# Gather steps beside the gates: from the streamed blocks and ticks to two behind each gate piece

## The chip, the core and the metric

The kernel runs on one core of a Trainium2 chip. TensorE (PE) does matrix products and transposes, VectorE (DVE) and ScalarE (ACT) the elementwise work, GpSimd (POOL) issues the gathers, SyncE (SP) and ACT issue the other transfers. Each engine takes its instructions in the order in which the program holds them, and waits where one of them needs something that another engine or a transfer has not yet delivered. The metric is the time of one execution on the device in microseconds (us), of which the median of three runs is compared.

## What is computed

Two layers of a decoder work on 512 prompt tokens and 64 sample tokens of width 1024. A layer is a mixer (a gated recurrence beside a short convolution, after one input projection and before one output projection) and a retrieval block, which is what the change touches. Cut to that block:

```
def peer(h, w_q, sub_keys, u_tab, v_tab):          # per 128 tokens
    q = (xb @ w_q).reshape(tb, PEER_HEADS, 2, D_KEY_HALF)
    s = jnp.einsum('thpd,hpkd->thpk', q, sub_keys)
    sv, si = lax.top_k(s, TOPK)
    ...
    fv, fi = lax.top_k(cand, TOPK)
    idx = jnp.take_along_axis(cand_idx, fi, axis=-1)     # 8 heads x 16 of 16384 experts
    g = jax.nn.softmax(fv, axis=-1)
    act = jax.nn.gelu(jnp.einsum('thkd,td->thk', u_tab[idx], xb))
    return jnp.einsum('thk,thkd->td', g * act, v_tab[idx])

    x = x + g1[:, None, :] * (merged @ w_out)
    x = x + g2[:, None, :] * peer(hn2, peer_w_q, peer_sub_keys, peer_u, peer_v)
```

Every token takes 128 of 16384 rows of a table u, forms a dot product with each, and adds up 128 rows of a table v with the weights that come of it. Both tables are 64 MB for a layer.

## The kernel before, in words

The tokens go two ways. For 384 prompt tokens the block is **dense**: all 16384 rows of u and of v are streamed as 128 blocks of 128 rows, the products of all rows with all tokens are formed, and a gate matrix that is zero outside the chosen rows picks what counts. The other 128 prompt tokens and the 64 sample tokens are **gathered**: a step fetches 128 rows of 4 KB by their indices with one indirect transfer that POOL issues (L659, tiles urs and vrs for the samples, urp and vrp for the prompt tokens, all of one ring of five buffers), and one DVE instruction uses them: a dot product (L665) or a weighted sum (L681; the first of a sum at L679). A layer has 64 + 64 steps of the samples and 128 + 128 of the prompt tokens, and behind the last sum stands finish (pf, L733, and x, L736), which adds the result to the stream x.

The retrieval block of a layer has these stages:

- the queries, and then the **u stage**: 72 streamed blocks, lo_u_0 to lo_u_71. Each block is split into a high and a low part (hi on ACT at L132, lo on DVE at L133) and multiplied by PE (pu, L712, 24 products). Three buffers hold raw pairs of blocks, four the parts.
- within the u stage, beside the stream, dense_slots turns the top-k lists into slots (three calls of combine, all DVE), and phase_a forms the gate matrix in 24 gate pieces of 4 quarters. A quarter is two DVE comparisons (oh, L944), two DVE products (A, L949), eight PE products (pgm, L954) and a copy (stg, L956); a piece ends with a transfer to DRAM (gd, L958), which ACT issues. In layer 0 the weights of the next layer's modulation are streamed in the same stage (raw_ada, pm).
- phase_b: 128 blocks of v (lo_v), the first 56 of which with a block of u each (lo_ub). Per block DVE applies the gates (L1047, from gt, read back from gd) and splits the result (h2l, L1050), and PE forms 18 products (pvo, L1018). The products of the last four blocks are held back to the end.
- the **tail**: the queue of gather steps is flushed, then finish, the sums of squares (L223), the transposed output (pyt, L1072) and its addition to x (L1075). In layer 0 the next mixer follows, whose projection weights are lo_wi; in layer 1 the last norm and y (L1109).

The gather steps stand in a queue, gtasks. pump(n) adds n to a credit and issues a step for each whole unit; issue_after(anchor[0]) places the step's DVE work on DVE behind one named instruction. That was, until now, the last split of a streamed block:

```
anchor[0] = V.tensor_tensor(out=lo, in0=raw, in1=hi.bitcast(F32), op=ALU.subtract).ins
```

The gate pieces are issued in the program between two pairs of streamed blocks, several at a time, but with a priority of their own, and the order on each engine is fixed when the program is built: the tie says behind which instruction a step stands at the earliest, not how soon. MPUMP, ARATE and BPUMP say how many steps the mixer, the gates and the two parts of phase_b release.

Of the kernel before, what the change touches and what calls it, by code (L numbers as in the profile page):

```python
# [71 lines left out]
def hybrid_step(ctx: ExitStack, tc: tile.TileContext, xT, cT, wada, vecs, fnorm, win, wout, wq, swin, swout, swq, subk,  # L72
# [835 lines left out]
    def dense_slots(l, pk, svd, sid, sl, ends):  # L908

        for t in range(NT):  # L910
            ii, jj, gg, gl = (pk.tile([P, P], F32, tag=n, bufs=2, name=f"{n}d{l}_{t}") for n in ("ii", "jj", "gg", "gl"))
            gh = pk.tile([P, P], F16, tag="gh", bufs=2, name=f"ghd{l}_{t}")
            combine(pk, svd[t].rearrange("p (h a) k -> p h a k", a=2), sid[t].rearrange("p (h a) k -> p h a k", a=2),
                    8, f"d{l}_{t}", gg.rearrange("p (h k) -> p h k", h=8), ii, jj, lambda us: pump(ARATE * us),
                    gscale=GS, bufs=2)
            V.tensor_copy(gh, gg)
            V.tensor_tensor(out=gl, in0=gg, in1=gh, op=ALU.subtract)
            V.tensor_tensor(out=gg, in0=gg, in1=gl, op=ALU.subtract)
            pt = small(f"ptd{l}_{t}")
            with tc.issue_after(ends[TIES[t]]):  # L920
                for n, s_ in enumerate((ii, jj, gg, gl)):
                    PE.transpose(pt[:, n * P:(n + 1) * P], s_, ident)
            S.activation(sl[t].rearrange("p a b -> p (a b)"), pt, AF.Copy)

    def phase_a(l, pg, pc, pa, sl, gd, activations, spilled):

        def tick(us):
            pump(ARATE * us)

        def slot(t, a, c0):  # L930

# [2 lines left out]
        def gate_piece(t, ch):  # L934
# [4 lines left out]
            for q in range(4):  # L939
# [6 lines left out]
                    oh.append(o)  # L946
                A = pa.tile([P, 2, 2, P, 2], F16, tag="A", bufs=2, name=f"A{l}_{t}_{c0}")
                for z in range(2):
                    V.tensor_tensor(out=A[:, z], in0=oh[0], in1=slot(t, 2 + z, c0), op=ALU.mult)  # L949
                    tick(0.6)  # L950
                pgm = bank(f"pgm{l}_{t}_{ch}_{q}")
                for n in range(4):
                    for z in range(2):
# [238 lines left out]
```

## Time and profile before

| what | value |
|---|---|
| median of three runs | 3724.26 us (3721.86, 3724.26, 3724.54) |
| profiled execution | 3732.58 us, of which the span of the trace is 3730.8 us |
| mean granted TensorE clock | 0.957 of full speed |
| PE busy | 3504.9 us, 94% |
| DVE busy | 2953.0 us, 79% |
| POOL busy | 1150.0 us, 31% |
| moved by all transfers | 1032.60 MB, mean 277 GB/s |

The profiled execution took 8.3 us more than the median. All starts and durations of the trace belong to it.

### The profile page before, as it was taken

How to read it: one execution, taken by the hardware profiler on the slowest of the kernel's cores; microseconds unless marked ns; L12 is line 12 of the kernel's file. 1: busy time of each engine (PE TensorE's matmuls, PEld its weight loads, DVE VectorE, ACT ScalarE, POOL GpSimd, SP SyncE). 2: the span in 40 equal slices, each digit the busy share in tenths (PEclk: the TensorE clock that was granted, in tenths of full speed). 3: DMA queues.
4: the chain of work that ended last, by engine and by line, in shares of the span. 5: the costliest groups of instructions: out<-in, count | busy, mean ns of one | idle time of the engine just before them, and what ended most of it. 6: DMA issues, size and time to landing. Idle time of an engine off the chain costs nothing.

```text
span 3730.8 us, 51432 instructions
## 1 busy us (share of the span) xinstructions
PE 3504.9 (94%) x18606; PEld 2926.0 (78%) x18606; DVE 2953.0 (79%) x6160; ACT 1483.6 (40%) x2027; POOL 1150.0 (31%) x830
## 2 busy tenths in 40 slices
PE   7989889978999999999988998899988999999998
PEld 4557668967889999888864576789976899998887
DVE  4327899999877888888863488899999688888887
ACT  3324334434563333333333344434446433333333
POOL 0001530043105555453300046200630155544431
PEclk9999989988999999999989999899986999999999
DMA  7765863479889999899846668424995799999994
GB/s 288 276 247 199 290 224 105 148 270 361 329 317 342 330 342 342 315 357 361 323 150 241 229 244 310 167 88 172 340 353 196 245 336 346 341 341 333 360 339 175
DMA packets 329648, 1032.60 MB, mean 277 GB/s; under 512 B 47152, under 2 KB 152752, under 8 KB 265904
## 3 DMA queue, kind: packets, MB, share of 16 engines
q1 hardware_dynamic: 203824, 554.25, 40.7%
q0 software_dynamic: 110592, 402.70, 30.1%
q10 hardware_dynamic: 14976, 72.36, 4.7%
q8 instruction: 146, 2.39, 0.2%
q14 instruction: 110, 0.90, 0.1%
HBM read 954.01 MB, written 75.15 MB: 276 GB/s over the span
## 4 chain that ended last, share of the span: by engine, by line
PE 64%; DVE 17%; DMA 7%; issue 6%; POOL 3%; ACT 3%; SPq 1%; DVEq 0%; POOLq 0%; ACTq 0%
PE pvo L1018 25%; PE pu L712 22%; PE pj L149 8%; POOL urs L659 3%; DMA gt<-gd 3%; PE pgm L954 1%; DMA raw_wi<-in_win_dram 1%; DVE A L949 1%; DVE lo_u L133 1%; DVE oh L944 1%; PE po L149 1%; PE pq L870 1%; PE pm L185 1%; DMA urs<-in_utab_dram,gidxs 1%; DVE accs L681 1%
## 5 line engine op out<-in xcount | busy, mean ns | idle before, releaser
L659 POOL DMA_INDIRECT urp<-in_utab_dram,gidx x256 | 383.8, 1499 | 639.5 <-DVE dot L665 405.7
L659 POOL DMA_INDIRECT vrp<-in_vtab_dram,gidx x256 | 384.1, 1500 | 494.2 <-DVE accp L681 460.8
L1018 PE MATMUL pvo<-hi_v,h2h 128*128 128x512 f32 x1536 | 482.1, 391 | 6.0 <-ACT h2h L1049 6.0
L1018 PE MATMUL pvo<-lo_v,h2h 128*128 128x512 f32 x1536 | 479.6, 391 | 0.7 <-DVE lo_v L133 0.7
L1018 PE MATMUL pvo<-hi_v,h2l 128*128 128x512 f32 x1536 | 456.9, 391 | 5.0 <-DVE h2l L1050 5.0
L712 PE MATMUL pu<-h2h,hi_u 128*128 128x384 f32 x1152 | 397.9, 345 | 7.0 <-ACT hi_u L132 4.9
L659 POOL DMA_INDIRECT vrs<-in_vtab_dram,gidxs x128 | 203.1, 1587 | 636.3 <-DVE smd L833 371.5
L712 PE MATMUL pu<-h2h,lo_u 128*128 128x384 f32 x1152 | 393.5, 343 | 1.0 <-DVE lo_u L133 1.0
L712 PE MATMUL pu<-h2l,hi_u 128*128 128x384 f32 x1152 | 394.0, 342 | 0.0
L659 POOL DMA_INDIRECT urs<-in_utab_dram,gidxs x128 | 172.7, 1349 | 690.9 <-PE pj L149 309.9
L133 DVE TENSOR_TENSOR lo_v<-raw_v,hi_v 128x1024 fp32r<-128x1024 f32 x256 | 313.0, 1223 | 67.8 <-ACT hi_v L132 66.8
L149 PE MATMUL pj<-hnh,hi_wi 128*128 128x512 f32 (+1 forms) x800 | 322.4, 404 | 33.9 <-ACT hi_wi L132 16.8
L1018 PEld LDWEIGHTS pvo<-hi_v,h2l 128*128 128x128 f32 x1536 | 289.0, 188 | 67.2 <-DVE h2l L1050 6.7
L1018 PEld LDWEIGHTS pvo<-lo_v,h2h 128*128 128x128 f32 x1536 | 289.1, 188 | 62.5 <-DVE lo_v L133 1.2
L1018 PEld LDWEIGHTS pvo<-hi_v,h2h 128*128 128x128 f32 x1536 | 288.3, 188 | 63.3 <-ACT h2h L1049 6.8
L681 DVE SCALAR_TENSOR_TENSOR accp<-vrp,dot,accp 128x1024 f32<-128x1024 f32 x252 | 323.3, 1283 | 1.8 <-DMA vrp<-in_vtab_dram,gidx 0.8
L149 PE MATMUL pj<-hnl,hi_wi 128*128 128x512 f32 (+1 forms) x800 | 316.8, 396 | 4.2 <-DVE hnl L280 4.2
L149 PE MATMUL pj<-hnh,lo_wi 128*128 128x512 f32 (+1 forms) x800 | 315.0, 396 | 0.1
L665 DVE CUSTOM_DVE_ANT_0 urp<-urp,xt 128x1024 f32<-128x1024 f32 x256 | 304.6, 1220 | 1.3 <-DMA urp<-in_utab_dram,gidx 1.3
L712 PE MATMUL pu<-h2h,lo_ub 128*128 128x384 f32 x896 | 300.1, 335 | 0.0
L712 PE MATMUL pu<-h2h,hi_ub 128*128 128x384 f32 x896 | 299.8, 335 | 0.0
L712 PE MATMUL pu<-h2l,hi_ub 128*128 128x384 f32 x896 | 299.7, 334 | 0.0
(440 smaller groups left out, 7185.7 us busy)
## 6 DMA issues: line engine op xcount, KB each, us to landing
raw_v<-in_vP_dram SPq DMA_DIRECT2D x128, 1024.0 KB
raw_u<-in_uT_dram SPq DMA_DIRECT2D x72, 1024.0 KB
raw_ub<-in_uT_dram SPq DMA_DIRECT2D x56, 1024.0 KB
raw_wi<-in_win_dram SPq DMA_DIRECT2D x48, 1024.0 KB
gd<-stg ACTq DMA_DIRECT2D x48, 1024.0 KB
gt<-gd SPq DMA_DIRECT2D x768, 64.0 KB
raw_ada<-in_wada_dram SPq DMA_DIRECT2D x43, 1024.0 KB
ad<-ao ACTq DMA_DIRECT2D x56, 384.0 KB
```

The source lines that it names most:

```text
L133: anchor[0] = V.tensor_tensor(out=lo, in0=raw, in1=hi.bitcast(F32), op=ALU.subtract).ins
L149: PE.matmul(out[:, c0:c1], a[:, w], b[:, k, c0:c1], start=(k == 0 and a is hi and b is xh), stop=(k == KT - 1 and a is lo))
L185: PE.matmul(pm[j * 32:(j + 1) * 32, 0:256], c32[:, k, :], raw[k // 4][:, j * 256:(j + 1) * 256], start=(k < 4), stop=(k >= 4))
L659: G.indirect_dma_start(out=rt, out_offset=None, in_=tab, in_offset=bass.IndirectOffsetOnAxis(ap=self.gidx[:, g, h, k:k + 1], axis=0))
L665: V.tensor_tensor_reduce(out=ur, in0=ur, in1=self.xt[g], scale=1.0, scalar=0.0, op0=ALU.mult, op1=ALU.add, accum_out=self.dot[:, g, h, k:k ...
L681: V.scalar_tensor_tensor(out=self.acc[g], in0=vr, scalar=w, in1=self.acc[g], op0=ALU.mult, op1=ALU.add)
L712: ends[i] = PE.matmul(pu[:, 0:TD], a[:, w], b[:, 0:NT, k, :], start=(k == 0 and a is hi and b is h2h), stop=(k == KT - 1 and a is lo)).ins
L870: PE.matmul(pqs[:, t0 * P:t1 * P], a[:, w], b[:, t0:t1, k, :], start=(k == 0 and a is hi and b is h2h), stop=(k == KT - 1 and a is lo))
L944: V.tensor_tensor(out=o, in0=iota2.unsqueeze(1).to_broadcast([P, 2, P, 2]), in1=slot(t, a, c0), op=ALU.is_equal)
L949: V.tensor_tensor(out=A[:, z], in0=oh[0], in1=slot(t, 2 + z, c0), op=ALU.mult)
L954: PE.matmul(pgm[:, n * P:(n + 1) * P], oh[1][:, n // 2, :, n % 2], A[:, z, n // 2, :, n % 2], start=(z == 0), stop=(z == 1))
L1018: PE.matmul(pv[t][q], a[:, tk], b[:, q * 512:(q + 1) * 512], start=(n == 0 and a is wh and b is vh), stop=(n == P - 1 and a is wl))
```

## The change

Beside the gates the steps are no longer tied to the streamed blocks. The anchor is set by each A of a gate quarter, and a piece releases ARATE = 2.0 steps at its end, behind its last A and after its transfer is issued. The ticks inside the pieces and inside combine release none any more. In place of about 67 steps before (24 pieces of 8 ticks of 0.24, and those of combine), the stage releases 48; phase_b gets a slightly higher rate, 3.1 and 1.4 steps for a block in place of 3.0 and 1.3.

```
-MPUMP, QRATE, ARATE, BPUMP = 2.5, 0.0, 0.4, (3.0, 1.3)
+MPUMP, QRATE, ARATE, BPUMP = 2.5, 0.0, 2.0, (3.1, 1.4)
...
             combine(pk, svd[t].rearrange("p (h a) k -> p h a k", a=2), sid[t].rearrange("p (h a) k -> p h a k", a=2),
-                    8, f"d{l}_{t}", gg.rearrange("p (h k) -> p h k", h=8), ii, jj, lambda us: pump(ARATE * us),
+                    8, f"d{l}_{t}", gg.rearrange("p (h k) -> p h k", h=8), ii, jj, lambda us: None,
                     gscale=GS, bufs=2)
...
-        def tick(us):
-            pump(ARATE * us)
...
                 for z in range(2):
-                    V.tensor_tensor(out=A[:, z], in0=oh[0], in1=slot(t, 2 + z, c0), op=ALU.mult)
-                    tick(0.6)
+                    anchor[0] = V.tensor_tensor(out=A[:, z], in0=oh[0], in1=slot(t, 2 + z, c0), op=ALU.mult).ins
...
             S.dma_start(gd[t * 8 + ch], stg)
+
+            pump(ARATE)
```

The order of all engines moves with it. Three places on DVE matter here. In the names a number ahead of the arrow is the tile's; accp_1 is the sum of the second group of 64 gathered prompt tokens, vrp_1_h_k the rows of its head pair h and choice k, so that vrp_1_3_15 is the last step of a layer.

First the end of layer 1, from the split of the last streamed block lo_v_55. Before, the last step stood ahead of it:

```order
L681 SCALAR_TENSOR_TENSOR accp_1_29992<-vrp_1_3_14_31600,dot_19825,accp_1_29992 128x1024
L133 TENSOR_TENSOR lo_v_54_32041<-raw_v_48_3_32038,hi_v_54_32040 128x1024
L681 SCALAR_TENSOR_TENSOR accp_1_29992<-vrp_1_3_15_31628,dot_19825,accp_1_29992 128x1024
L1050 TENSOR_TENSOR h2l<-at_48_31913,h2h 128x384
L133 TENSOR_TENSOR lo_v_55_32048<-raw_v_48_3_32038,hi_v_55_32047 128x1024
L736 SCALAR_TENSOR_TENSOR x<-pf_1_31688,mod_6506,x 128x64 x8
L223 TENSOR_REDUCE ss<-sq_32055 128x128
```

Now (the first rows, and the last ones before finish):

```order
L133 TENSOR_TENSOR lo_v_54_32041<-raw_v_48_3_32038,hi_v_54_32040 128x1024
L681 SCALAR_TENSOR_TENSOR accp_1_30250<-vrp_1_2_8_31244,dot_19825,accp_1_30250 128x1024
L1048 TENSOR_TENSOR h2l<-at_48_31913,h2h 128x384
L133 TENSOR_TENSOR lo_v_55_32048<-raw_v_48_3_32038,hi_v_55_32047 128x1024
L681 SCALAR_TENSOR_TENSOR accp_1_30250<-vrp_1_2_9_31272,dot_19825,accp_1_30250 128x1024
L681 SCALAR_TENSOR_TENSOR accp_1_30250<-vrp_1_2_10_31275,dot_19825,accp_1_30250 128x1024
...
L681 SCALAR_TENSOR_TENSOR accp_1_30250<-vrp_1_3_14_31786,dot_19825,accp_1_30250 128x1024
L681 SCALAR_TENSOR_TENSOR accp_1_30250<-vrp_1_3_15_31814,dot_19825,accp_1_30250 128x1024
L736 SCALAR_TENSOR_TENSOR x<-pf_1_31817,mod_6446,x 128x64 x8
```

Behind lo_v_55 stand 23 steps, vrp_1_2_9 to vrp_1_3_15, where none stood.

Then the end of layer 0, around the second split of the next mixer's weights, lo_wi_0_1. Before:

```order
L133 TENSOR_TENSOR lo_wi_0_0_16724<-raw_wi_0_0_16721,hi_wi_0_0_16723 128x1024
L681 SCALAR_TENSOR_TENSOR accp_1_14535<-vrp_1_3_11_16062,dot_3787,accp_1_14535 128x1024
L681 SCALAR_TENSOR_TENSOR accp_1_14535<-vrp_1_3_12_16090,dot_3787,accp_1_14535 128x1024
L681 SCALAR_TENSOR_TENSOR accp_1_14535<-vrp_1_3_13_16120,dot_3787,accp_1_14535 128x1024
L681 SCALAR_TENSOR_TENSOR accp_1_14535<-vrp_1_3_14_16148,dot_3787,accp_1_14535 128x1024
L133 TENSOR_TENSOR lo_wi_0_1_16807<-raw_wi_0_0_16721,hi_wi_0_1_16806 128x1024
L681 SCALAR_TENSOR_TENSOR accp_1_14535<-vrp_1_3_15_16178,dot_3787,accp_1_14535 128x1024
L736 SCALAR_TENSOR_TENSOR x<-pf_1_16181,mod_168,x 128x64 x8
```

Now:

```order
L133 TENSOR_TENSOR lo_wi_0_0_16724<-raw_wi_0_0_16721,hi_wi_0_0_16723 128x1024
L681 SCALAR_TENSOR_TENSOR accp_1_14800<-vrp_1_2_3_15643,dot_3787,accp_1_14800 128x1024
L681 SCALAR_TENSOR_TENSOR accp_1_14800<-vrp_1_2_4_15646,dot_3787,accp_1_14800 128x1024
L681 SCALAR_TENSOR_TENSOR accp_1_14800<-vrp_1_2_5_15676,dot_3787,accp_1_14800 128x1024
L133 TENSOR_TENSOR lo_wi_0_1_16807<-raw_wi_0_0_16721,hi_wi_0_1_16806 128x1024
L681 SCALAR_TENSOR_TENSOR accp_1_14800<-vrp_1_2_6_15704,dot_3787,accp_1_14800 128x1024
L681 SCALAR_TENSOR_TENSOR accp_1_14800<-vrp_1_2_7_15764,dot_3787,accp_1_14800 128x1024
...
L681 SCALAR_TENSOR_TENSOR accp_1_14800<-vrp_1_3_15_16339,dot_3787,accp_1_14800 128x1024
L736 SCALAR_TENSOR_TENSOR x<-pf_1_16369,mod_168,x 128x64 x8
```

Behind lo_wi_0_1 stand 26 steps, vrp_1_2_6 to vrp_1_3_15, in place of one.

Last the u stage of layer 1, around lo_u_61, behind which the trace of before has its longest pause between two blocks. The first number of oh and A is the group of 128 tokens (0 to 2), the second the slot, four to a quarter. Before:

```order
L665 ISA urp_0_0_4_24365,dot_19825<-urp_0_0_4_24365,xt_0_20202 128x1024
L944 TENSOR_TENSOR oh_0_84_22944<-iota_83,sl_0_19826 128x512
L133 TENSOR_TENSOR lo_u_61_25492<-raw_u_30_25459,hi_u_61_25491 128x1024
L949 TENSOR_TENSOR A_0_80_22929<-oh_0_80_22925,sl_0_19826 128x512 x2
L944 TENSOR_TENSOR oh_0_84_22942<-iota_83,sl_0_19826 128x512
L949 TENSOR_TENSOR A_0_84_22946<-oh_0_84_22942,sl_0_19826 128x512 x2
...
```

Now:

```order
L946 TENSOR_TENSOR A_1_60_23440<-oh_1_60_23436,sl_1_19827 128x512 x2
L681 SCALAR_TENSOR_TENSOR accs_0_19138<-vrs_0_2_6_23454,dots_17897,accs_0_19138 128x1024
L941 TENSOR_TENSOR oh_1_64_23527<-iota_83,sl_1_19827 128x512
L941 TENSOR_TENSOR oh_1_64_23525<-iota_83,sl_1_19827 128x512
L133 TENSOR_TENSOR lo_u_61_25426<-raw_u_30_25393,hi_u_61_25425 128x1024
L941 TENSOR_TENSOR oh_1_68_23544<-iota_83,sl_1_19827 128x512
```

When this block is split the gates have come to slot 64 of the second group in place of slot 80 of the first, 28 quarters further, and the steps are still those of the samples. Up to lo_u_62 there now follow 50 oh, 52 A and 13 steps, where 106 oh, 108 A and 12 steps stood; the gates begin behind lo_u_33 in place of lo_u_43. In layer 0 the order is the same up to lo_u_22; between lo_u_23 and lo_u_36 there are now 169 oh and A and 20 steps, where 109 and 44 stood, and from lo_u_36 on 15 quarters fewer are left. Up to lo_v_55 phase_b holds 231 steps of layer 0 in place of 235.

## Rows read from the trace of the kernel before

**Rows 1.** The page: the chain that ended last, shares of the span by engine.

```profile
PE 64%; DVE 17%; DMA 7%; issue 6%; POOL 3%; ACT 3%; SPq 1%; DVEq 0%; POOLq 0%; ACTq 0%
```

**Rows 2.** Busy time in stretches; ends, length, each engine, granted clock, DMA.

```profile
core 0: us, PE busy (x) PEld busy (x) DVE busy (x) ACT busy (x) POOL busy (x), PEclk, DMA share, GB/s
755.70:896.30 140.60, 106.31 (x703) 90.27 (x701) 133.71 (x250) 53.18 (x67) 67.79 (x44) 0.81 0.86 308
896.30:1110.00 213.70, 209.59 (x1704) 184.04 (x1703) 170.23 (x365) 121.19 (x156) 23.68 (x21) 0.97 0.89 336
...
2690.00:2771.00 81.00, 79.09 (x555) 74.52 (x554) 77.25 (x126) 43.58 (x52) 29.12 (x25) 1.00 0.95 360
2771.00:2868.70 97.70, 68.47 (x454) 47.16 (x455) 92.03 (x240) 56.48 (x56) 13.03 (x13) 0.55 0.61 230
2868.70:2948.00 79.30, 79.30 (x571) 75.10 (x570) 56.69 (x113) 49.59 (x60) 5.11 (x3) 1.00 0.56 202
3450.00:3650.00 200.00, 200.00 (x892) 165.89 (x891) 167.91 (x207) 74.15 (x98) 77.43 (x52) 1.00 0.96 355
```

**Rows 3.** SP queue, a pair of u blocks in layer 0.

```profile
882.85 0.33 SPq L140 DMA_DIRECT2D raw_u<-in_uT_dram  x1
```

**Rows 4.** DVE in order of time, the first block of that pair.

```profile
896.29 1.21 DVE L133 TENSOR_TENSOR lo_u<-raw_u,hi_u 128x1024 fp32r<-128x1024 f32 x1
```

**Rows 5.** DVE groups by form from 2771 to 2868.7.

```profile
L944 DVE TENSOR_TENSOR oh<-iota,sl 128x512 f16<-128x512 f16 x107 | 41.3, 422 | 3.7 <-PE pgm L954 3.4
L949 DVE TENSOR_TENSOR A<-oh,sl 128x512 f16<-128x512 f16 x108 | 41.2, 423 | 1.5
L665 DVE CUSTOM_DVE_ANT_0 urp<-urp,xt 128x1024 f32<-128x1024 f32 x12 | 14.5, 1215 | 0.0
...
L665 DVE DVE_READ_ACCUMULATOR2_ANT dot<- 128x1 f32 x12 | 1.0, 79 | 0.0
```

**Rows 6.** PE groups by form from 2868.7 to 2948.

```profile
L954 PE MATMUL pgm<-A,oh 128*128 128x128 f16 x192 | 17.3, 221 | 0.0
```

**Rows 7.** DVE in order of time, four sums in a row, layer 0.

```profile
1882.17 5.24 DVE L681 SCALAR_TENSOR_TENSOR accp<-vrp,dot,accp 128x1024 f32<-128x1024 f32 x4
```

**Rows 8.** DVE in order of time, end of layer 0.

```profile
1890.55 1.23 DVE L133 TENSOR_TENSOR lo_wi<-raw_wi,hi_wi 128x1024 fp32r<-128x1024 f32 x1 [3.13 <-ACT hi_wi L132]
1891.69 1.28 DVE L681 SCALAR_TENSOR_TENSOR accp<-vrp,dot,accp 128x1024 f32<-128x1024 f32 x1
1895.06 1.62 DVE L736 SCALAR_TENSOR_TENSOR x<-pf,mod,x 128x64 f32<-128x64 f32 x8 [2.09 <-PE pf L733]
1897.80 1.94 DVE L223 TENSOR_REDUCE ss<-sq 128x128 f32<-128x1024 f32 x1 [1.12 <-ACT sq L221]
```

**Rows 9.** DVE in order of time, end of layer 1.

```profile
3687.95 1.28 DVE L681 SCALAR_TENSOR_TENSOR accp<-vrp,dot,accp 128x1024 f32<-128x1024 f32 x1
...
3689.66 1.23 DVE L133 TENSOR_TENSOR lo_v<-raw_v,hi_v 128x1024 fp32r<-128x1024 f32 x1
...
3698.71 2.00 DVE L223 TENSOR_REDUCE ss<-sq 128x128 f32<-128x1024 f32 x1 [1.13 <-ACT sq L221]
3704.44 2.16 DVE L1075 SCALAR_TENSOR_TENSOR x<-pyt,mod,x 128x128 f32<-128x128 f32 x8 [3.72 <-PE pyt L1072]
3708.06 2.16 DVE L1075 SCALAR_TENSOR_TENSOR x<-pyt,mod,x 128x128 f32<-128x128 f32 x8 [1.46 <-PE pyt L1072]
```

**Rows 10.** PE in order of time, end of layer 1: the last held product.

```profile
3706.95 0.63 PE L1018 MATMUL pvo<-hi_v,h2l 128*128 128x512 f32 x2
```

**Rows 11.** The tile vrs, its transfers from issue to landing.

```profile
DMA to landing us min/median/max: 4.2/7.1/15.9
```

**Rows 12.** The tile vrp, its transfers from issue to landing.

```profile
DMA to landing us min/median/max: 4.4/7.8/12.6
```

**Rows 13.** PE in order of time, the first product of phase_b in layer 1.

```profile
2963.23 1.22 PE L1018 MATMUL pvo<-hi_v,h2h 128*128 128x512 f32 x2 [4.74 <-ACT h2h L1049]
```

**Rows 14.** ACT queue, the last gate transfers of layer 1.

```profile
2928.97 0.33 ACTq L958 DMA_DIRECT2D gd<-stg  x1
```

## The prediction, made before the changed kernel ran

> **What bounds the kernel now.** I read the chain that ended last first: PE holds 64% of it and DVE 17% [rows 1]. That is an average, so I cut the span by the stages that the change touches [rows 2]. The reader is to see three kinds of stretch. In phase_b PE is never idle (200.00 of 200 us from 3450), while DVE has 32 us to spare beside 52 gathers. There a step costs nothing. Between lo_u_23 and lo_u_36 of layer 0 (755.7 to 896.3) DVE is busy 133.71 of 140.6 us and PE only 106.31, at a granted clock of 0.81; between lo_u_61 and lo_u_62 of layer 1 (2771 to 2868.7) DVE is busy 92.03 of 97.7 us, PE 68.47 at 0.55. There DVE sets the pace and each step costs its length. The third kind is the two tails, where nothing is left that could cover a step: in layer 0 finish waits for the sum that starts at 1891.69 [rows 8]; in layer 1 the last sum starts at 3687.95, and PE still forms held products until 3707.6 [rows 9, 10].
>
> **What the change does, part by part.**
>
> *The work itself.* All 389 tasks of a layer's queue remain, with the same transfers. The price of a step is only the place where it stands.
>
> *Gates of layer 0.* Between lo_u_23 and lo_u_36, 24 steps leave and 60 oh and A come in (the order, above). A step takes DVE some 1.2 us among other work (1.28 less the 0.09 by which neighbours overlap, as lo_wi and the sum behind it do [rows 8]). For an oh or A, in the stretch of layer 1: 92.03 us less 12 dot products of 14.5, their 1.0 of reading out and one split of 1.2 leaves 75.3 us for 215, 0.35 us each [rows 2, 4, 5]. So −24 × 1.2 + 60 × 0.36 = −7. From lo_u_36 on PE is the bound (209.59 of 213.7 us), and it has 15 quarters fewer there. A quarter is 8 pgm: 192 of them sum to 17.3 us [rows 6], 0.72 us a quarter, an upper value since such products overlap; I take 0.6, so −9. Against it: in the new order the modulation products pm that free a raw buffer stand directly ahead of pu_36, and that pair of u blocks is loaded only then. Before, the transfer issued at 882.85 gave lo_u_36 at 896.29 [rows 3, 4], 13.4 us, half of it covered by gates; I put the uncovered half on, +7. Layer 0: −9, with ends −20 (no stall, 0.72 a quarter) and +5 (the whole 13.4 uncovered and nothing gained behind).
>
> *Gates of layer 1.* Behind lo_u_61 DVE now has 102 oh and A and 13 sums where it had 214 and 12 dot products: 102 × 0.35 + 13 × 1.28 + 1.2 + 2.7 (the 5.7 us of idle time, in proportion) = 56 us instead of 97.7, −41. The 28 quarters have not gone: they stand ahead of lo_u_61, where DVE (77.25 of 81) and PE (79.09 of 81) are both nearly full [rows 2]. On PE they cost 28 × 0.6 = +17; on DVE 112 × 0.35 less some 17 steps that left this stretch, 39 − 20 = +19; I take +18. Last, the gates end later in the order, some 5.5 instead of 7.3 blocks of u before the first product of phase_b. That product already waits 4.74 us at 2963.23, because gt can only be read when the last gd, issued at 2928.97, is written [rows 13, 14]: 1.8 blocks of 24 products each, some 4 us, are +7. Layer 1: −16, with ends −28 (the moved quarters hidden by half, no later gt) and −3.
>
> *Phase_b.* It holds 231 steps of layer 0 up to lo_v_55 for 235, at 3.8 us a step [rows 2]. PE is the bound, DVE has room: 0. What phase_b does not hold goes to the tails.
>
> *Tail of layer 0.* Behind lo_wi_0_1 stand 26 steps for 1: 25 more on the path to finish. What is a step worth where nothing else is left? The sums depend on each other: four in a row took 5.24 us, 1.31 each [rows 7]; this is the floor. But the ring has five buffers. Five rows lie ready; from then on a buffer comes free, POOL issues (I put 0.3 us), the rows land, and the sum takes 1.31. Landing is 7.1 us in the median for vrs, 7.8 for vrp, 4.2 at the least [rows 11, 12]. By 7.1 a round is 8.7 us for five steps, 1.74 each; by 7.8 and 0.65 on POOL it is 1.95; by 4.2 it would be 1.16, and DVE's 1.31 holds. I take 1.74, since the 7.8 was measured under phase_b's full stream (DMA share 0.96), which a tail does not have. 5 × 1.31 + 21 × 1.74 − 1.28 = +42; ends +33 and +46. PE idles meanwhile; there is no work of the next mixer that does not need x.
>
> The Trainium skill gives another price for such a transfer. In "DMA: Bandwidth & Descriptors", section "Anatomy of one DMA — SWDGE (gpsimd) path", it is a fixed 2.0 us and the bytes at 436 GB/s; for 512 KB that is an estimate of 3.2 us, by which five buffers would never hold DVE up and both tails would cost their floors. The least landing of this trace, 4.2 us, is already above it [rows 11].
>
> *Tail of layer 1.* 23 steps stand behind lo_v_55, which ends at 3690.8; none before. By the same prices the last sum ends at 3690.8 + 5 × 1.31 + 18 × 1.74 = 3728.7. From the end of the last sum to L223 it took 4.8 us in layer 0 (1892.97 to 1897.80) [rows 8]; from L223 to the end of the span 32.1 us in layer 1, of which 3.72 and 1.46 were waits for output that hung on the held products [rows 9]. These are long done by then (3707.6), so 26.9 remain: 3728.7 + 4.8 + 26.9 = 3760.4, against 3730.8: +30. Ends: +22 by 1.31 a step, +33 by 1.95. Of the 38 us that the steps take, 17 lie beside held products: that is why this tail costs less for its steps than the other.
>
> **Sum.** −9 − 16 + 42 + 30 = +47 us on the profiled execution, 3732.58 to 3779.6. That execution lies 8.3 us above the median of the runs, 3724.26, and I put the difference on the median: **3771 us**. What a measurement of this kernel can tell from no change is about 0.2%, 7.4 us.
>
> **The rivals.**
>
> *A: the tails at DVE's pace.* If rows land within 5.2 us of a free buffer, a step costs 1.31: tails +33 + 22, gates −25, +30: 3754. For it speaks the minimum of 4.2 us; against it the medians of 7.1 and 7.8, both well over 5.2. Chance 0.25. By the rule of the Trainium skill named above it would come out like this.
>
> *B: gathers alone are slower.* With one sort of traffic, 4 KB pieces in random places, landing might stay at 7.8 or above, or PE, after idling 40 us and at a granted clock like the 0.55 above, might be late in what follows: 1.95 to 2.2 a step and some us behind each tail, +60: 3784. For it speaks that 1.74 us for 512 KB means 300 GB/s by gathers alone, of 355 GB/s in all in the fullest stretch. Chance 0.15.
>
> *C: faster.* The gates win more than the tails lose. The place is the stretch that DVE binds in both layers: if the blocks of u run on without the pauses there, layer 0 gives its −20 and layer 1 the whole −41, and PE's 106 us in layer 0, which had a granted clock of 0.81, become 86: another −20, −81 in all. It decides from the point where the gates win more than the tails' floor of 55 and the 7.4 that can be told. At −81 + 55 the time is −26: 3698. For it speaks that low clock; against it that PE is full ahead of these stretches and behind them, so that what moves out of them is paid there. Chance 0.05.
>
> *D: no change.* The steps could run earlier than the order suggests. They cannot: DVE takes its instructions in order, so 26 and 23 sums stand behind the last split whatever the pace before. Only the gates' gain could meet the tails' floor, at −50 + 55: 3729. Chance 0.05.
>
> **How the numbers follow.** My forecast, tails between 1.5 and 1.9 us a step, has 0.5. With A and B on the same side, slower has 0.9, same 0.05, faster 0.05. The range leaves out C, D and the outer half of A and B: low is the tails' floor with the gates a little better than I take them (+55 − 42 = +13), 3737; high is both tails at their upper ends and the gates at half their gain (+79 − 13 = +66), 3790.
>
> **What would show it.** In the profile after: behind the last lo_v of each layer a row of sums on DVE, each of which waits for the landing of vrp, with 26 of them over some 43 us in layer 0 and 23 over 38 in layer 1; PE idle there. The stretch from lo_u_61 to lo_u_62 should shrink to some 56 us and the one ahead of it grow by 18; that of layer 0 from lo_u_23 to lo_u_36 should be about as long as before. If the sums wait for nothing, A is right. If they stand a pitch of 2 us or more apart, B. I am wrong altogether if the stage of the gates gains over 50 us, or if PE proves to have had work left in the tails.

## The result, and the profile after

The changed kernel takes 3765.64 us (median of 3758.37, 3762.09, 3769.18 and 3770.74), the kernel before 3724.4 beside it: a ratio of 1.0104, 95% interval 1.0086 to 1.0122, **41 us slower**. The forecast was 3771, with a range of 3737 to 3790. Experiments 8 and 11 below have one execution each at a much lower granted clock (3992.67 us at 0.825 and 5794.82 us at 0.553), and their medians leave it out (the 3736 in what I expected of experiment 12 has it in).

The profiled execution of the change has a span of 3768.9 us, 38.1 above that of before. In stages, first the windows that answer to [rows 2] (gates of layer 0 from lo_u_23 to lo_u_36 and on to the first lo_v; gates of layer 1 from lo_u_23 to lo_u_61, and the pause to lo_u_62; the second of [rows 2] ends at 1110, short of the first lo_v), then the two tails:

```profile
core 0: us, PE busy (x) PEld busy (x) DVE busy (x) ACT busy (x) POOL busy (x), PEclk, DMA share, GB/s
758.00:897.40 139.40, 114.12 (x796) 96.81 (x794) 126.80 (x284) 66.30 (x79) 25.93 (x21) 0.81 0.71 255
897.40:1133.00 235.60, 226.35 (x1739) 202.10 (x1739) 160.76 (x304) 119.14 (x157) 35.18 (x28) 0.97 0.91 334
2632.10:2817.70 185.60, 184.38 (x1288) 173.15 (x1286) 167.28 (x333) 105.94 (x128) 40.31 (x23) 1.00 0.77 273
2817.70:2874.40 56.70, 35.76 (x230) 26.25 (x231) 53.37 (x118) 27.32 (x29) 16.13 (x14) 0.58 0.75 265
1885.60:1927.40 41.80, 0.45 (x2) 0.03 (x1) 33.36 (x27) 0.00 (x0) 26.62 (x21) 0.54 0.84 291
3696.50:3733.80 37.30, 14.04 (x62) 11.28 (x61) 29.55 (x24) 0.00 (x0) 24.47 (x19) 0.75 0.82 285
```

The pause in layer 1 has shrunk from 97.7 to 56.7 us. The stretch of layer 0 that DVE binds is 139.4 us long where it was 140.6. The last two windows are new: PE is busy 0.45 of 41.8 us in the one and 14.04 of 37.3 in the other. What stands there, on DVE in order of time, end of layer 0 (answers to [rows 8]):

```profile
1884.46 1.23 DVE L133 TENSOR_TENSOR lo_wi<-raw_wi,hi_wi 128x1024 fp32r<-128x1024 f32 x1 [4.16 <-ACT hi_wi L132]
1885.60 7.91 DVE L681 SCALAR_TENSOR_TENSOR accp<-vrp,dot,accp 128x1024 f32<-128x1024 f32 x6
1895.12 1.28 DVE L681 SCALAR_TENSOR_TENSOR accp<-vrp,dot,accp 128x1024 f32<-128x1024 f32 x1 [1.60 <-DMA vrp<-in_vtab_dram,gidx]
1897.03 6.57 DVE L681 SCALAR_TENSOR_TENSOR accp<-vrp,dot,accp 128x1024 f32<-128x1024 f32 x5 [0.63 <-DMA vrp<-in_vtab_dram,gidx]
...
1924.84 2.60 DVE L681 SCALAR_TENSOR_TENSOR accp<-vrp,dot,accp 128x1024 f32<-128x1024 f32 x2 [0.81 <-DMA vrp<-in_vtab_dram,gidx]
1931.21 1.62 DVE L736 SCALAR_TENSOR_TENSOR x<-pf,mod,x 128x64 f32<-128x64 f32 x8 [3.77 <-PE pf L733]
1933.95 1.94 DVE L223 TENSOR_REDUCE ss<-sq 128x128 f32<-128x1024 f32 x1 [1.12 <-ACT sq L221]
```

and end of layer 1 (answers to [rows 9]):

```profile
3695.36 1.22 DVE L133 TENSOR_TENSOR lo_v<-raw_v,hi_v 128x1024 fp32r<-128x1024 f32 x1
3696.50 5.24 DVE L681 SCALAR_TENSOR_TENSOR accp<-vrp,dot,accp 128x1024 f32<-128x1024 f32 x4
3702.01 1.28 DVE L681 SCALAR_TENSOR_TENSOR accp<-vrp,dot,accp 128x1024 f32<-128x1024 f32 x1 [0.28 <-DMA vrp<-in_vtab_dram,gidx]
...
3731.16 2.61 DVE L681 SCALAR_TENSOR_TENSOR accp<-vrp,dot,accp 128x1024 f32<-128x1024 f32 x2 [1.21 <-DMA vrp<-in_vtab_dram,gidx]
3737.53 1.63 DVE L736 SCALAR_TENSOR_TENSOR x<-pf,mod,x 128x64 f32<-128x64 f32 x8 [3.77 <-PE pf L733]
3740.28 1.94 DVE L223 TENSOR_REDUCE ss<-sq 128x128 f32<-128x1024 f32 x1 [1.12 <-ACT sq L221]
```

The first four or six sums follow each other without a pause, 1.31 us each; they find their rows landed. Then most of them wait for vrp. From 1885.60 to 1927.44 there are 26 sums in 41.8 us, from 3696.50 to 3733.77 there are 23 in 37.3: 1.61 and 1.62 us each, the ready rows at the start included. PE sees the first of these tails as one wait, for the last sum, ahead of pf:

```profile
1927.50 3.67 PE L733 MATMUL pf<-eye,accp 128*128 128x64 f32 x16 [41.45 <-DVE accp L681]
```

The first product of phase_b in layer 1 waits 7.78 us for the gates, where it waited 4.74 [rows 13]:

```profile
2975.01 1.22 PE L1016 MATMUL pvo<-hi_v,h2h 128*128 128x512 f32 x2 [7.78 <-ACT h2h L1047]
```

For the experiments I cut each trace at the same splits. This table is worked out from the starts of lo_u_22, the first and the last lo_v and lo_wo's last, and from the spans; before in us, the others as differences to it. One execution of each kernel stands in it, and the executions of one kernel differ by 10 to 30 us, so single entries under 5 us say little. Experiments 5 and 6 had one execution each, and the one that was profiled of experiment 10 (3714.12 us) is the fastest of its ten, so these three are left out.

| stage | before | change | 1 | 2 | 3 | 4 | 7 | 8 | 9 | 11 | 12 |
|---|---|---|---|---|---|---|---|---|---|---|---|
| start to lo_u_22, layer 0 | 752.6 | +2.2 | 0.0 | −3.0 | +44.7 | +3.2 | +0.9 | −2.0 | +2.9 | −2.9 | +2.9 |
| gates 0: to the first lo_v | 378.9 | −0.7 | −16.0 | +28.5 | +22.7 | −6.8 | −4.4 | −26.0 | −8.5 | +34.5 | −14.0 |
| phase_b 0: to the last lo_v | 745.5 | −7.0 | −3.5 | −1.9 | −5.1 | +76.1 | −4.4 | −4.4 | +8.9 | −3.6 | +4.0 |
| tail 0 and mixer 1: to lo_wo | 495.7 | +38.8 | +30.6 | −11.0 | −13.6 | −21.6 | +40.1 | +27.6 | −5.7 | −5.4 | −5.9 |
| to lo_u_22, layer 1 | 223.9 | −0.9 | −1.2 | −1.3 | +46.4 | −0.9 | −1.2 | −1.1 | +0.3 | −4.5 | +1.3 |
| gates 1: to the first lo_v | 343.1 | −26.5 | −19.6 | −13.4 | −25.7 | −26.5 | −18.0 | −20.2 | −17.7 | +3.0 | −17.7 |
| phase_b 1: to the last lo_v | 750.0 | −0.2 | −9.7 | +28.1 | +4.5 | +86.5 | −10.8 | −9.7 | +0.3 | +15.5 | −0.1 |
| tail 1: to the end | 41.1 | +32.4 | +31.9 | +0.5 | −2.7 | −2.6 | +34.1 | +31.9 | +0.4 | +0.1 | +1.3 |
| sum (span) | 3730.8 | +38.1 | +12.5 | +26.4 | +71.2 | +107.5 | +36.3 | −3.8 | −19.2 | +36.6 | −28.3 |

### The profile page after: what moved, and what is told of

Its sections match the earlier page's. It is cut to its first block, busy times and chain, and to the rows that moved or that the text cites. A ratio compares the mean times of both kernels' runs of the same rounds, so it can differ in the third digit from the quotient of the medians.

```text
span 3768.9 us, 51444 instructions
## 1 busy us (share of the span) xinstructions
PE 3495.0 (93%) x18606; PEld 2922.0 (78%) x18606; DVE 2958.4 (78%) x6160; ACT 1482.2 (39%) x2027; POOL 1061.5 (28%) x830
## 4 chain that ended last, share of the span: by engine, by line
PE 66%; DVE 14%; DMA 6%; issue 6%; POOL 4%; ACT 3%; SPq 0%; POOLq 0%; DVEq 0%; ACTq 0%
PE pu L712 26%; PE pvo L1016 22%; PE pj L149 8%; POOL urs L659 2%; POOL vrp L659 2%; PE po L149 2%; PE pgm L950 2%; DMA raw_wi<-in_win_dram 1%; PE pq L870 1%; DMA urs<-in_utab_dram,gidxs 1%; DVE oh L941 1%; DVE A L946 1%; DMA vrp<-in_vtab_dram,gidx 1%; PE pm L185 1%; DVE urs L665 1%
## 5 line engine op out<-in xcount | busy, mean ns | idle before, releaser
L659 POOL DMA_INDIRECT vrp<-in_vtab_dram,gidx x256 | 366.0, 1430 | 465.2 <-DVE accp L681 429.2
L659 POOL DMA_INDIRECT vrs<-in_vtab_dram,gidxs x128 | 176.8, 1381 | 1019.7 <-DVE accs L681 530.5
L659 POOL DMA_INDIRECT urp<-in_utab_dram,gidx x256 | 338.1, 1321 | 426.0 <-DVE dot L665 337.0
L133 DVE TENSOR_TENSOR lo_v<-raw_v,hi_v 128x1024 fp32r<-128x1024 f32 x256 | 312.7, 1221 | 53.5 <-ACT hi_v L132 49.3
```

The costliest lines, as they stand in the source:

```text
L659: G.indirect_dma_start(out=rt, out_offset=None, in_=tab, in_offset=bass.IndirectOffsetOnAxis(ap=self.gidx[:, g, h, k:k + 1], axis=0))
```

## The experiments

**1: the old ties, but as few steps as the change releases.** My theory after the result: the number of steps that is left for the tails is the loss. The rival: the new tie itself.

```
-MPUMP, QRATE, ARATE, BPUMP = 2.5, 0.0, 0.4, (3.0, 1.3)       # kernel before
+MPUMP, QRATE, ARATE, BPUMP = 2.5, 0.0, 0.286, (3.1, 1.4)
```

> The kernel before, with its own ties (streamed blocks, ticks), but releasing only as many steps beside the gates as the changed kernel (47 of 65 in each layer) and with the new rates of phase_b. Its order leaves 31 and 23 steps for the two tails. If the number left for the tails costs the time (my theory), it is as slow as the changed kernel: +74 us in the tails, −15 to −35 beside the gates for 18 fewer steps in each layer, 3755 to 3780. If the new tie costs the time (the rival), this kernel has none of it and stays within 10 us of 3724.

Measured: 3750.15 us, ratio 1.0074 (1.0050 to 1.0097). Both tails are there (+31.9 in layer 1; in layer 0 the part from lo_wi_0_1 to the next lo_wi is 89.5 us for 49.6), and the gates won 16 and 20 us. So the tails' loss needs no new tie. But it came out 5 us below the range that I gave it, and 15 below the change.

**2: the new tie, with as many steps as before beside the gates.**

```
-MPUMP, QRATE, ARATE, BPUMP = 2.5, 0.0, 2.0, (3.1, 1.4)       # changed kernel
+MPUMP, QRATE, ARATE, BPUMP = 2.5, 0.0, 2.8, (3.0, 1.3)
```

> The changed kernel, still with two-sided ties behind the gates' A, but 2.8 steps for a piece in place of 2.0 and the old rates of phase_b: 66 and 63 steps beside the gates, 3 and 0 in the tails. If the count is the cause, the tails' +74 go away and with them most of what the gates won: 3710 to 3735. If the tie is the cause, it stays above 3750.

Measured: 3764.38 us, ratio 1.0107 (1.0066 to 1.0149). My theory falls in its strict form: the tails are gone (+0.5 in layer 1, −11.0 with the mixer in layer 0) and the kernel is as slow as the change. The loss has moved to the gates of layer 0 (+28.5) and the begin of phase_b in layer 1 (+28.1), where PE waits for the gates (PE's waits: us in total, times, longest):

```profile
PE pvo L1016 <- ACT h2h L1047: 23.5, 1, 23.5
```

The gates have moved here too: 181 oh and A stand between lo_u_23 and lo_u_36 of layer 0, 109 in the kernel before, and that stretch takes 152.6 us for 140.6.

**3: the mixers take the steps.**

```
-MPUMP, QRATE, ARATE, BPUMP = 2.5, 0.0, 2.0, (3.1, 1.4)
+MPUMP, QRATE, ARATE, BPUMP = 3.5, 0.0, 2.0, (3.1, 1.4)
```

> The changed kernel, with the mixer releasing 3.5 steps at each call in place of 2.5: 104 and 112 steps ahead of the u stage (74 and 80 before), 47 beside the gates, none in either tail. If only the place of the steps matters, the gates keep their gain (−8 and −27 with phase_b), the tails cost nothing (−8 against the kernel before too), and the mixers pay what DVE cannot hide, 0 to 36 us in layer 0, where DVE is nearly full, and less in layer 1: 3685 to 3720. By the tie theory 3750 or more.

Measured: 3798.61 us, ratio 1.0189 (1.0170 to 1.0209); a miss. There are no tails, but the steps did not land in the mixer. They pile up on DVE ahead of the queries: +44.7 and +46.4 us there. Of the sums between 530 and 690, and of PE behind them:

```profile
L681 DVE SCALAR_TENSOR_TENSOR accs<-vrs,dots,accs 128x1024 f32<-128x1024 f32 x33 | 42.3, 1282 | 8.1 <-DMA vrs<-in_vtab_dram,gidxs 7.6
```

```profile
PE pvb L239 <- DVE ss L217: 43.9, 1, 43.9
```

The kernel before waited here for

```profile
PE pvb L239 <- DVE ss L217: 4.5, 1, 4.5
```

33 sums in a row that nothing covers, 1.28 us each and some waits for rows, are a third tail. The gates of layer 0 lose another 22.7 us: 209 oh and A stand ahead of lo_u_36 there.

**4: phase_b at a higher rate.**

```
-MPUMP, QRATE, ARATE, BPUMP = 2.5, 0.0, 2.0, (3.1, 1.4)
+MPUMP, QRATE, ARATE, BPUMP = 2.5, 0.0, 2.0, (4.0, 2.0)
```

> The changed kernel with 4.0 and 2.0 steps for a block of phase_b in place of 3.1 and 1.4. Its order has no step in the tails but 61 and 66 of them within the 8 blocks where phase_b passes from pairs of u and v blocks to v alone, where 14 stood. If a step costs about 1.6 us wherever more stand than the blocks cover, those 47 and 52 surplus steps stall the blocks by some 30 to 50 us in each layer, and little is won: 3735 to 3780. If only the tails proper cost time, and phase_b hides any step, it is 3685 to 3700.

Measured: 3850.54 us, ratio 1.0337 (1.0317 to 1.0357). The stall is there, but twice as large as I said, +76 and +87 us. The windows of the two places, DVE's sums in the first, and what PE waits for there:

```profile
core 0: us, PE busy (x) PEld busy (x) DVE busy (x) ACT busy (x) POOL busy (x), PEclk, DMA share, GB/s
1572.00:1656.00 84.00, 12.46 (x57) 12.46 (x58) 64.17 (x59) 1.44 (x2) 62.39 (x49) 0.53 0.91 321
3391.00:3507.00 116.00, 35.73 (x177) 32.86 (x176) 93.95 (x92) 10.47 (x15) 83.00 (x61) 0.65 0.93 331
```

```profile
L681 DVE SCALAR_TENSOR_TENSOR accp<-vrp,dot,accp 128x1024 f32<-128x1024 f32 x48 | 61.7, 1286 | 19.8 <-DMA vrp<-in_vtab_dram,gidx 19.0
```

```profile
PE pf L733 <- DVE accp L681: 73.7, 1, 73.7
```

48 sums and 84 us: PE stands at pf, which needs the first group's last sum, and every product behind pf waits with it. I had counted on the products of those 8 blocks as cover; in PE's order they stand behind pf. So neither here nor ahead of the queries does a heap of sums cost less than in the tails. The edit of BPUMP in the change itself, 3.1 and 1.4 for 3.0 and 1.3, moves no step: with either the order holds 231 and 233 steps in phase_b and 31 and 23 in the tails.

**5 and 6: what sets the pace of a tail.** I had worked it out from the ring of five buffers. The trace after seems to say otherwise. POOL in the middle of layer 1's tail:

```profile
3708.12 1.40 POOL L659 DMA_INDIRECT vrp<-in_vtab_dram,gidx  x1 [0.30 <-issue]
3709.82 1.49 POOL L659 DMA_INDIRECT vrp<-in_vtab_dram,gidx  x1 [0.30 <-issue]
3711.61 1.01 POOL L659 DMA_INDIRECT vrp<-in_vtab_dram,gidx  x1 [0.30 <-issue]
```

It starts each gather 0.30 us after the one before, with no buffer named as what it waited for. If POOL is the bound, the ring's size does not matter.

```
-ROWS = 5                        # experiment 5, changed kernel
+ROWS = 4

-RAWS, HIS = 3, 4                # experiment 6, changed kernel
-ROWS = 5
+RAWS, HIS = 3, 3
+ROWS = 6
```

> The changed kernel with a ring of 4 row buffers in place of 5; 31 and 24 steps in the tails. If the ring sets the pace of a tail (a round of some 8 us shared by its buffers, as I predicted), a step of the tails takes about 8.0/4 = 2.0 us instead of 1.62. If POOL sets it (in the trace after, most of the gathers of layer 1's tail start 0.30 us after the one before them, with no wait for a buffer, about 1.6 us apart), it stays at 1.6.

> The changed kernel with 6 row buffers, and, to make room for them, 3 buffers for the parts of a block in place of 4 (so the time of the whole is not compared, only the tails): 22 and 14 steps stand behind the last lo_v. If the ring sets the pace, a step of the tails falls to DVE's 1.31 us and no sum waits for its rows. If POOL sets it, it stays near 1.6 once the rows that lay ready are used up.

Measured by one execution each, DVE in order of time, end of layer 1. With four buffers:

```profile
3743.24 2.60 DVE L681 SCALAR_TENSOR_TENSOR accp<-vrp,dot,accp 128x1024 f32<-128x1024 f32 x2
3746.52 2.66 DVE L681 SCALAR_TENSOR_TENSOR accp<-vrp,dot,accp 128x1024 f32<-128x1024 f32 x2 [0.68 <-DMA vrp<-in_vtab_dram,gidx]
3750.60 1.28 DVE L681 SCALAR_TENSOR_TENSOR accp<-vrp,dot,accp 128x1024 f32<-128x1024 f32 x1 [1.42 <-DMA vrp<-in_vtab_dram,gidx]
...
3787.10 1.28 DVE L681 SCALAR_TENSOR_TENSOR accp<-vrp,dot,accp 128x1024 f32<-128x1024 f32 x1 [0.22 <-DMA vrp<-in_vtab_dram,gidx]
```

With six:

```profile
3686.19 9.24 DVE L681 SCALAR_TENSOR_TENSOR accp<-vrp,dot,accp 128x1024 f32<-128x1024 f32 x7
3695.68 1.28 DVE L681 SCALAR_TENSOR_TENSOR accp<-vrp,dot,accp 128x1024 f32<-128x1024 f32 x1 [0.24 <-DMA vrp<-in_vtab_dram,gidx]
3697.20 7.92 DVE L681 SCALAR_TENSOR_TENSOR accp<-vrp,dot,accp 128x1024 f32<-128x1024 f32 x6 [0.24 <-DMA vrp<-in_vtab_dram,gidx]
```

With four, 24 sums take 45.1 us and in layer 0 26 take 49.3: 1.88 and 1.90 each. With six, 14 take 18.9 and in layer 0 17 take 23.7: 1.35 and 1.40, and two and four of them wait, for 0.5 and 1.5 us in all, where I had expected no wait. With five it was 1.61 and 1.62. These means hold the first sums, whose rows lay ready. A round of the ring, from the start of a sum to the start of the sum that next uses its buffer, is 7.7 and 7.8 us in the mean with four buffers (1.93 a step), 8.3 in both tails with five (1.66) and 8.3 and 8.5 with six, where DVE's own 1.31 is nearly reached. The ring sets the pace. POOL's starts follow it: in the two tails of the change a gather starts 1.11 or 1.12 us after the end of the sum that freed its buffer in 32 of 39 cases, and 0.27 us in the other seven. The whole kernels took 3824.41 us (experiment 5) and 3742.41 (experiment 6), the kernel before 3720.67 beside them.

**7 and 8: which part of the new tie.** The change does two things at once: no step is released in combine, and the anchor is A. Experiment 7 keeps the anchor and gives combine its steps back, experiment 8 the reverse.

```
-                    8, f"d{l}_{t}", ..., ii, jj, lambda us: None,                 # experiment 7
+                    8, f"d{l}_{t}", ..., ii, jj, lambda us: pump(0.286 * us),
-MPUMP, QRATE, ARATE, BPUMP = 2.5, 0.0, 2.0, (3.1, 1.4)
+MPUMP, QRATE, ARATE, BPUMP = 2.5, 0.0, 1.375, (3.1, 1.4)

-                    anchor[0] = V.tensor_tensor(out=A[:, z], in0=oh[0], in1=slot(t, 2 + z, c0), op=ALU.mult).ins
+                    V.tensor_tensor(out=A[:, z], in0=oh[0], in1=slot(t, 2 + z, c0), op=ALU.mult)     # experiment 8
```

> The changed kernel, with its tie behind the gates' A, but some 15 of its 47 steps released in combine again (as in the first experiment), the rest two-thirds as many behind each piece; 31 and 24 steps in the tails. The first experiment, with the old ties, the same count and the same tails, was some 15 us faster than the change, and its trace gained them between lo_u_22 and the first lo_v of layer 0 (−16 us against −1). If what costs there is that no step stands beside combine any more, where PE was busy 32.70 of 32.70 us and covered nine of them, this kernel gets the 15 us back: 3745 to 3757, the stage of layer 0 at −10 or better. If the anchor on A costs it, it stays at 3760 to 3770.

> The changed kernel without its new anchor: two steps are still released at the end of each piece and none in combine, but they are tied to the last streamed block again. 48 steps in each u stage and 31 and 23 in the tails, as in the change. If the steps missing beside combine cost the time, it is as slow as the change, 3758 to 3772; if the anchor on A does, it falls to the first experiment's 3745 to 3755.

Measured: 7 takes 3764.00 us, ratio 1.0095 (1.0067 to 1.0122), 8 takes 3733.99, ratio 1.0025 (1.0008 to 1.0042), 11 us below the range that I gave it. My second theory falls too: steps beside combine win nothing back, and the one line of the anchor is worth about 30 us. Experiment 8 is also some 16 us faster than experiment 1, which has the same anchor, nearly the same count and the same tails, but releases its steps in the ticks and in combine. So releasing them at the end of a piece seems to be worth something too; no run changed that alone. The stages say where: gates of layer 0, −0.7 with the anchor, −26.0 without, and phase_b of layer 1, −0.2 and −9.7. In experiment 8, DVE between lo_u_35 and lo_u_36 of layer 0 (832.4 to 868), and the windows of that pause and of all behind it to the first lo_v:

```profile
L681 DVE SCALAR_TENSOR_TENSOR accs<-vrs,dots,accs 128x1024 f32<-128x1024 f32 x12 | 15.4, 1280 | 0.6 <-DMA vrs<-in_vtab_dram,gidxs 0.6
L941 DVE TENSOR_TENSOR oh<-iota,sl 128x512 f16<-128x512 f16 x27 | 10.9, 420 | 0.1
L946 DVE TENSOR_TENSOR A<-oh,sl 128x512 f16<-128x512 f16 x28 | 10.7, 422 | 0.1
```

```profile
832.40:868.00 35.60, 27.66 (x212) 21.15 (x210) 34.72 (x72) 15.77 (x20) 16.41 (x13) 0.69 0.92 348
868.00:1103.40 235.40, 227.73 (x1819) 200.50 (x1819) 177.86 (x360) 133.18 (x170) 34.51 (x25) 0.99 0.89 335
```

27 oh and 28 A stand in a pause of 35.6 us. The change has 54 and 54 in one of 60.7 us, and PE idles a third of it:

```profile
836.70:897.40 60.70, 40.32 (x295) 28.92 (x294) 56.25 (x126) 29.49 (x32) 16.18 (x14) 0.64 0.80 277
L941 DVE TENSOR_TENSOR oh<-iota,sl 128x512 f16<-128x512 f16 x54 | 20.6, 418 | 1.1 <-PE pgm L950 0.8
L946 DVE TENSOR_TENSOR A<-oh,sl 128x512 f16<-128x512 f16 x54 | 20.5, 420 | 0.5
```

From lo_u_23 to lo_u_36 it is 114.3 us and 108 oh and A without the anchor, 139.4 and 169 with it; behind lo_u_36 PE has 15 quarters fewer and the time is the same, 235.4 and 235.6 us.

**11: the anchor alone, in the kernel before.**

```
-                    V.tensor_tensor(out=A[:, z], in0=oh[0], in1=slot(t, 2 + z, c0), op=ALU.mult)
+                    anchor[0] = V.tensor_tensor(out=A[:, z], in0=oh[0], in1=slot(t, 2 + z, c0), op=ALU.mult).ins
```

> The kernel before with one line of the change alone: the steps are anchored on each A of the gates; ticks, combine, rates and count as before (65 steps in each u stage, 4 and 0 in the tails). Its order has 166 oh and A and 40 steps between lo_u_22 and lo_u_36 of layer 0, where the kernel before has 109 and 44, the change 169 and 20, and the eighth experiment 108 and 24. If it is the anchor that pulls 15 quarters of gates ahead of lo_u_36, where PE has nothing to do beside them, that stage of layer 0 gets 20 to 30 us longer, with no tail to blame: 3740 to 3765. If the anchor does harm only together with the fewer steps, it stays within 8 us of 3724.

Measured: 3768.13 us, ratio 1.0116 (1.0089 to 1.0144), just above what I expected. With no tail and with the former count, one line makes the kernel as slow as the whole change does. The same pause (854.5 to 918.9), the same views, and the first product of phase_b in layer 1:

```profile
L949 DVE TENSOR_TENSOR A<-oh,sl 128x512 f16<-128x512 f16 x56 | 21.7, 419 | 0.6
L944 DVE TENSOR_TENSOR oh<-iota,sl 128x512 f16<-128x512 f16 x55 | 21.2, 418 | 3.8 <-PE pgm L954 3.5
L681 DVE SCALAR_TENSOR_TENSOR accs<-vrs,dots,accs 128x1024 f32<-128x1024 f32 x13 | 16.6, 1277 | 0.0
```

```profile
854.50:918.90 64.40, 42.85 (x309) 31.78 (x308) 56.78 (x128) 30.69 (x33) 16.09 (x13) 0.63 0.74 256
918.90:1163.10 244.20, 229.14 (x1739) 201.55 (x1740) 160.58 (x318) 121.36 (x159) 27.55 (x25) 0.97 0.86 318
```

```profile
2998.96 1.22 PE L1018 MATMUL pvo<-hi_v,h2h 128*128 128x512 f32 x2 [17.77 <-ACT h2h L1049]
```

The pause is 64.4 us long, with 111 oh and A in it, and PE idles a third of it. The later gates end later against phase_b in layer 1: the first product waits 17.77 us for them.

**9, 10 and 12: a version that is faster.** A longer ring takes steps into phase_b, since more rows are on the way, and makes a tail's step cheaper. The room comes from one of the four buffers for the parts of a block.

```
-RAWS, HIS = 3, 4
-ROWS = 5
+RAWS, HIS = 3, 3
+ROWS = 7          # 9: in experiment 1; 10: in the kernel before; 12: in experiment 8
```

> The first experiment (old ties, 47 steps beside the gates) with a ring of 7 row buffers, and 3 buffers for the parts of a block in place of 4 to make room. The order of phase_b now holds 253 and 252 steps, and 10 and 5 are left for the tails in place of 31 and 23. If the tails are the loss and their pace the ring's, 21 steps of 1.62 and the faster pace of the rest leave in layer 0 (−36), 18 in layer 1 (−25), so 3750 − 61 = 3689, with some us more for the missing block buffer: 3685 to 3710, faster than the kernel before. If phase_b does not hide the added steps, 3735 or more.

> The kernel before with the ring of 7 and 3 block buffers: 65 steps beside the gates, 245 and 239 in phase_b, none in the tails. It tells what of the former kernel's time the ring alone is worth: its 6 steps in the tail of layer 0 are −8 to −10, the rest should stay: 3712 to 3722. If the block buffer that is missing costs more than that, it is slower than 3724.

> The eighth experiment (the change without its anchor) with the ring of 7 row buffers and 3 block buffers of the ninth: 48 steps beside the gates, 251 and 252 in phase_b, 11 and 4 in the tails. From the first to the ninth experiment this ring took 46 us off the median; off the eighth's 3736 that gives 3690: 3678 to 3706, the fastest here. If the ring and the steps' new places don't add up, it stays near the ninth's 3704 or above.

Measured: 9 takes 3703.71 us, ratio 0.9937 (0.9914 to 0.9959); 10 takes 3729.96, ratio 1.0012 (1.0000 to 1.0023), a miss of 8 us; 12 takes 3703.98, ratio 0.9949 (0.9931 to 0.9967), at the upper end of the range that I gave it. Both 9 and 12 are faster than the kernel before by 20 us, and as fast as each other: the 16 us between experiments 1 and 8 do not add to the ring, as the second reading of what I expected of 12 has it. The ring, with the block buffer given up for it, is worth nothing by itself, as 10 shows: it needs the fewer steps beside the gates. It is the count of the change with the longer ring that wins, without the anchor on A (which was not run with seven buffers): in 9 the tails are −5.7 and +0.4 instead of +30.6 and +31.9, and the gates keep −8.5 and −17.7. Phase_b of layer 0 pays 4 to 9 us.

## Why the prediction was right, point by point

**Tail of layer 0**, forecast +42: from the start of lo_wi_0_1 to L223 it was 7.25 us [rows 8] and is 49.49 (1884.46 to 1933.95), **+42.2**. The price of a step behind the five ready rows was 1.74 by a round of 8.7 us; the trace has 1.66, a round of 8.3. Inside the round two errors went against each other: landing was put at 7.1 us, and the time between a free buffer and POOL's start at 0.3. In the trace of the change 6.0 us pass in the mean from POOL's start to the sum that uses the rows, and 1.0 from the end of a sum to POOL's start. Landing itself is on record in the same tails of experiment 8, layer 0 and layer 1:

```profile
DMA to landing us min/median/max: 5.0/5.9/6.1
DMA to landing us min/median/max: 5.2/5.9/6.5
```

The total is closer still by luck: the sums took 41.8 us for 43.1, and pf took 3.67 us where 2.00 had stood (granted clock 0.50 for 1.00, its 1.2 GHz level for the 2.4 GHz one, after PE had waited 41 us). Experiments 5 and 6 show the ring as the cause. Rival A's 1.31 needed a round of 6.55 us, and none of the rounds' means came near it; with a sixth buffer the step comes near 1.31 all the same. By the Trainium skill ("DMA: Bandwidth & Descriptors", section "Anatomy of one DMA — SWDGE (gpsimd) path"), whose fit I had estimated at 3.2 us for such a transfer, five buffers would have been enough for that; the trace does not agree, as no row of these tails landed in less than 5.0 us.

**Tail of layer 1**, forecast +30: from the start of the last lo_v to the end 41.1 us before, 73.5 after, **+32.4**. PE's held products were indeed done long before: the last of them starts at 3709.93, and the last sum ends at 3733.77. The sums took 37.3 us for 37.9. What the forecast lacks is 1.7 us ahead of L223, pf at the lower clock again, and 1.8 us behind it (28.7 for 26.9).

**Gates of layer 1**, forecast −16, measured **−26.5** to the first lo_v. The terms: the pause behind lo_u_61 −41 and 56 us, measured −41.0 and 56.7. The stretch ahead of it +18, measured +14.3 (lo_u_23 to lo_u_61, 171.4 to 185.7). The later gates +7, measured +3.0 of longer wait for the first product, which falls in phase_b. The mechanism was right in each term, and the two losses were sized 4 us too high each. The low end of this part, −28, does not follow from its own terms, −41 and half of 18, which give −32 (in layer 0 the ends −20 and +5 come out at −18 and +6); the range was not built on them.

**Gates of layer 0**, forecast −9, measured **−0.7**. The stretch to lo_u_36 was to stay about as long as before, and did (139.4 for 140.6). DVE's work there fell by 6.9 us (133.71 to 126.80) for the −7 of the forecast, and its idle time rose by 5.7 (6.9 to 12.6) for +7. But the load that I had named is the smaller part of that: DVE waits 2.56 us for lo_u_36, whose load is issued at 889.11.

```profile
897.39 1.22 DVE L133 TENSOR_TENSOR lo_u<-raw_u,hi_u 128x1024 fp32r<-128x1024 f32 x1 [2.56 <-ACT hi_u L132]
```

The rest is oh waiting for the products pgm, 5.0 us for 1.6, and for ptd, 3.0 for 1.3, which I had not counted. That these come to +7 is luck. The 9 us that I gave the stretch behind lo_u_36 did not come, and this is the term that failed: 235.6 us for 235.2, of which before

```profile
896.30:1131.50 235.20, 231.09 (x1834) 205.28 (x1833) 176.25 (x370) 132.83 (x170) 25.56 (x22) 0.98 0.88 329
```

PE's busy time fell by 4.7 us (231.09 to 226.35), half of what I took for the 15 quarters, and its idle time rose by as much (4.1 to 9.3): PE now waits 6.2 us for hi_u and 3.3 for lo_u, where it waited 1.5 and 0.7.

**Phase_b and the rest**, forecast 0: −7.0 and −0.2 in the two phases, and small differences in the mixers. The 235 steps that I gave the phase_b of layer 0 before are 239 in its order and in its trace, and 239 in layer 1: the change takes 8 and 6 steps out of it, in spite of the higher rates. They stand in the tails, whose 26 and 23 steps were counted in the order and are right. The sum of all stages is 38.1 us for the 47 of the forecast, on the median 41.

**What the sum hid.** It is right, and its gates, −25 forecast and −27 measured, look right as well. That is partly luck: the two layers' errors, +8 and −10, cancel. And I treated the gates as one effect and they are two, which the experiments took apart. Fewer steps beside the gates, released at the ends of the pieces, win: without the anchor, −26.0 and −20.2 us, and about −10 more in phase_b of layer 1 (experiment 8). The count alone, with the old places of release, wins −16.0 and −19.6 (experiment 1). The anchor on A gives nearly all of it back in layer 0: 15 quarters move ahead of lo_u_36, most of them into a pause in which PE has no block to work on. I had seen these 60 more oh and A in the order and had charged them to the steps that left, 24 for 60, as if one went with the other. They do not: with the anchor alone the gates move as far and only four steps leave. What I then believed from the result, that the tails alone were the loss, was wrong, as experiment 2 showed; so was the belief that steps put back beside combine would win the time back, as 7 and 8 showed. By experiments 8 and 11 together: the anchor costs 30 us in the change (3764 and 3766 with it, 3734 without) and 45 in the kernel before (3768 for 3723). The tails, some 74 us, less the gates' gain of 46 and phase_b's 14, are the rest, 14 us; the median of experiment 8 is 10 above the kernel before. Its one traced execution is 4 below it, since its mixer of layer 1 is some 15 us shorter. That the change and experiment 11 come out at the same 3765 to 3769 is chance.

**What stays open.** Why an anchor on A makes the order put the gates earlier was not tried; that it does is seen in the orders of four kernels (109 and 108 oh and A ahead of lo_u_36 without it, 169 and 166 with it). What the place of release is worth by itself (experiment 8 against 1) was not run alone. The mixer of layer 1 is 3 to 15 us shorter in several kernels with a long tail ahead of it, and no experiment was made on that.

## What to carry to other kernels

A deferred step is free only where another engine is both busy and not waiting for what stands behind the step; so count, in the order of the changed program, where the steps end that a new rule no longer places, and price those at the end of a stage at the pace of their ring. The handle is the ring: two buffers more (with one block buffer fewer) moved 18 to 21 steps of each layer into covered time, while higher rates only heaped the steps up in front of another wait. And where one edit changes a tie and a number, run each alone before believing the sum: here two opposite effects of 25 us each made a right total out of a half-understood stage.

## What the runs showed of the hardware that was not expected

A 512 KB gather, 128 rows of 4 KB, kept a ring's round of about 8 us (7.7 to 7.8 with four buffers, 8.3 with five) also where the stream of blocks had ended. The DMA engines were busy 0.82 to 0.84 of the time there, with the gathers nearly alone (21 gathers of 512 KB in 41.8 us are some 263 of 291 GB/s). Landing itself came down from a median of 7.5 us in phase_b to 5.9 in the tails (experiment 8, layer 0 and both tails), not to the least landing of before, 4.2 us. Sums that depend on each other stand 1.31 us apart, 1.28 of work and 0.03 between. And a "0.30 issue" ahead of each POOL gather does not mean that POOL is the limit: with one buffer more the same tail ran at 1.35 to 1.40 us a step.
